# An encoder block on one NeuronCore: in-place squares and low parts of x first in the opening, and the loads of h spread between the operand loads of the second FFN layer

## The chip, the cores and the metric

The kernel runs on one core of a Trainium2 chip. Its time is the device time of one execution, in microseconds (us). Of the kernel before there are three timed runs (1366.92, 1367.37 and 1368.26 us) and one profiled execution. A measurement of this kernel can tell a difference of about 0.2% (2.7 us) from none.

The engines are TensorE (PE, matrix products; its weight loads are listed apart as PEld), VectorE (DVE), ScalarE (ACT), GpSimd (POOL) and SyncE (SP, which here issues all the DMAs). Each engine works through its own list of instructions in the order in which the program issues them; an instruction whose inputs are not there holds up everything behind it on that engine.

## The reference

One layer (DEPTH = 1) for x of 1024 tokens by 1024 features, all in float32:

```python
xn = rmsnorm(h, norm_mix[l]);  proj = xn @ w_in[l]          # q, k, v, u, vs, gates
att = chunked_rel_attention(q, k, v, att_rel_bias[l])
sgu = spatial_gating(gelu(u), gelu(vs), ...)
merged = gates[:, :, 0] * (att @ w_br_att[l]) + gates[:, :, 1] * (sgu @ w_br_sgu[l])
h = h + merged @ w_out[l]
g, up = split(rmsnorm(h, norm_ffn[l]) @ w_ffn_in[l], 2)
h = h + (silu(g) * up) @ w_ffn_out[l]
return rmsnorm(h, norm_final)
```

rmsnorm multiplies each token by the reciprocal root of the mean of its squares, and each feature by a gain.

## The kernel before

Activations lie with features on the 128 partitions and tokens along the row, so x is eight tiles x0 to x7 of 128 features by 1024 tokens (512 KB each). TensorE multiplies in a reduced format, so every operand is split into a high part (ScalarE copies it, rounded) and a low part (what is left, on VectorE or GpSimd), and each product is three matmuls: high by high, high by low, low by high.

**The opening (lines 278 to 431).** For each block x_k, `load_x` issues the load on SP, ScalarE makes the high part `xh` of x_k times the gain (line 289) and VectorE the low part `xl` (line 290). `square_x` makes the square of x_k in a tile of its own (ScalarE, or GpSimd for k = 2 and 3, lines 296 and 298), and VectorE adds it to `acc` (line 300). On VectorE the additions stand between the low parts: `xl` of block k, then the addition for block k-2. `load_first` loads the first weights of q and k in three pieces (blocks 0 and 1, 2 and 3, 4 to 7) and splits them, low parts on GpSimd. The weights of v are four pieces `wv` of two blocks each. They are loaded through the two buffers tagged `raw`, which the first weights of q and k hold until their low parts are made; the low parts of the first two pieces are made on GpSimd, those of the last two on VectorE. The load of x7 comes behind that of the first `wv` in SP's list.

TensorE first runs 18 transposes of nothing, then for each block k twelve matmuls of 512 columns (line 346): q and k, two halves of the tokens, three passes. From the second block on the order is pass by pass, the one with `xl` second. Then come the eight token tiles of v (line 356, 24 matmuls each, reading `wv` piece by piece). Within tile 0, after `SUM_AT` = 12 of its matmuls, TensorE sums `acc` over the partitions (`ss`, line 269, 16 instructions), and a short chain on VectorE and GpSimd (lines 254 to 262 and 411) makes the reciprocal root `rstd_tok`. Within tile 1, after `SPREAD_AT` = 8 matmuls, TensorE spreads it over the partitions (line 275), ScalarE copies it (line 416) and VectorE takes the finished q and k out of their PSUM banks (lines 374 and 376). Tile 2 of v uses the bank of `q0a`, the first half of q.

**The second FFN layer (lines 1507 to 1527).** The activations of the first layer went through DRAM (`act_dram`), the h of before the FFN too (`h_dram`), and the prepared weights as well (`g_dram`, 84 operands of 384 KB). The layer is one list `order_g` of 84 products, nine matmuls of 512 columns each. Operand i lies in one of six buffers; `prepare_g(i + 6)` in step i issues the load of operand i+5 (line 1433), which waits until product i-1 has read that buffer. Operands 0 to 5 and product 0 come earlier, within the first layer's last steps. Between that and the loop stand four loads of h, 1 MB each (line 1485), into a pool that takes the place of the first layer's. The results are added to h by `collect_g`; the first that does so is that of product 8. In steps 8 to 13 one load of 512 KB each brings the next six activations (`stage_act`, line 1399), from which VectorE, ScalarE and GpSimd make the next right-hand operands (lines 1416, 1419 and 172).

Of the kernel before, what the change touches and what calls it, by code (L numbers as in the profile page):

```python
# [11 lines left out]
F32 = mybir.dt.float32  # L12
F32R = mybir.dt.float32r
AF = mybir.ActivationFunctionType
OP = mybir.AluOpType

P = 128
D = 1024
S = 1024
KB = D // P  # L20
# [16 lines left out]
LOW_G = ((0, 1, 1, 1, 0, 1, 0, 1, 1, 1, 0, 1, 0, 1, 1, 1, 0, 1, 0, 1, 1), (1, 0, 0, 0, 0, 1, 1, 0, 1, 0, 0, 1, 0, 0, 1, 0, 1, 1, 0, 0, 1))  # L37
SHARES = (((4, 5), (4, 4)), ((4, 3), (4, 4)), ((4, 3), (6, 4)), ((4, 4), (3, 3)))
WAKE = 18
SUM_AT, SPREAD_AT = 12, 8  # L40
EPS = 1e-6
NEG = -1e30
GELU_A = 0.044715
# [4 lines left out]
def encoder_block(ctx: ExitStack, tc: tile.TileContext, xT, w_in, w_v, w_vs, w_att, w_sgu, w_out,  # L48
# [5 lines left out]
    nc = tc.nc  # L54
# [3 lines left out]
    wpool = ctx.enter_context(tc.tile_pool(name="wpool", bufs=2))  # L58
# [10 lines left out]
    def slot(name, shape=(P, S), dt=F32, pool=slots):  # L69
        return pool.tile(list(shape), dt, name=name, tag="slot")  # L70
# [4 lines left out]
    halves = (slice(0, HALF), slice(HALF, S))  # L75
# [145 lines left out]
    for j in range(PAIRS):  # L221
        qw[j] = block(f"wq{j}", w_in[j], D)
        kw[j] = block(f"wk{j}", w_in[4 + j], D)
        if j == 0:
            vw = [block(f"wv{i}", w_v[i], D, keep=two_slots, lo_engine=nc.vector if i >= 2 else None) for i in range(4)]
        for g in {1: (0,), 2: (1,), 3: (2, 3)}.get(j, ()):
            uw[g] = block(f"wu{g}", w_in[8 + g], D)
    gw, bw = [], {}
# [11 lines left out]
    g_mix, g_ffn, g_fin, b_gate = vec[:, 0:8], vec[:, 8:16], vec[:, 16:24], vec[:, 24:40]  # L240
# [35 lines left out]


    xg = []
    acc = slot("acc")

    def load_x(k, parts=1):

        x.append(slot(f"x{k}"))
        xg.append((slot(f"xh{k}", dt=F32R), slot(f"xl{k}", dt=F32R)))
        for s in halves if parts == 2 else (slice(0, S),):
            nc.sync.dma_start(x[k][:, s], xT[k * P:(k + 1) * P, s])
            yield 1
            hi, lo = (part[:, s] for part in xg[k])
            nc.scalar.activation(hi, x[k][:, s], AF.Copy, scale=g_mix[:, k:k + 1])
            nc.vector.scalar_tensor_tensor(lo, x[k][:, s], g_mix[:, k:k + 1], hi.bitcast(F32),  # L290
                                           op0=OP.mult, op1=OP.subtract)

    def square_x(k):
        q = acc if k == 0 else slot(f"xq{k}")
        if k in POOL_SQUARES:
            nc.gpsimd.tensor_tensor(out=q, in0=x[k], in1=x[k], op=OP.mult)
        else:
            nc.scalar.activation(q, x[k], AF.Square)
        if k:
            nc.vector.tensor_tensor(out=acc, in0=acc, in1=q, op=OP.add)  # L300

    def load_first(c0, c1):
        s = slice(c0 * P, c1 * P)
        for u in (qw[0], kw[0]):
            if c0 == 0:
                for part in ("raw", "hi", "lo"):
                    u[part] = wpool.tile([P, D], F32 if part == "raw" else F32R, name=u["name"] + part, tag=part)
            nc.sync.dma_start(u["raw"][:, s], u["src"][:, s])
        yield 1
        for u in (qw[0], kw[0]):  # L310
            hi, lo, raw = (u[part][:, s] for part in ("hi", "lo", "raw"))
            nc.scalar.copy(hi, raw)
            nc.gpsimd.tensor_tensor(out=lo, in0=raw, in1=hi.bitcast(F32), op=OP.subtract)
# [1 line left out]
    awake = wide_ps("awake", "s")[:, :P]  # L315
    warm = small.tile([P, 1], F32, name="warm", tag="warm", bufs=1)
    nc.scalar.activation(warm, ones, AF.Square)
    POOL_SQUARES = (2, 3)
    x = []
    first_x, first_w = load_x(0, 2), load_first(0, 2)  # L320
    next(first_x)
    next(first_w)
    next(first_x)
    drain(first_w, first_x, load_x(1), load_first(2, 4))
    for k in range(2, KB):
        drain(load_x(k))
        square_x(k - 2)
        if k == 2:
            drain(load_first(4, KB))
            state["dma"] = state["split"] = 2  # L330
        if k >= 6:
            split_to(k - 3)
    square_x(KB - 2)
    square_x(KB - 1)
    dma_to(6)
    split_to(6)


    for _ in range(WAKE):
# [1 line left out]
    first = [dense_ps("q0a"), dense_ps("q0b"), *(wide_ps(f"k0{n}", "v", (P, HALF)) for n in "ab")]  # L341
    for k in range(KB):
        of_k = [(i, half, n) for i in range(2) for n in range(3) for half in range(2)]
        for i, half, n in of_k if k else sorted(of_k, key=lambda x: x[1]):
            w, b = passes((qw, kw)[i][0], k, xg[k])[n]
            nc.tensor.matmul(first[2 * i + half], w, b[:, halves[half]], start=k == 0 and n == 0,
                             stop=k == KB - 1 and n == 2)

    def project(ps, pieces, t):

# [5 lines left out]
                nc.tensor.matmul(ps, a, b, start=k == 0 and n == 0, stop=k == KB - 1 and n == 2)  # L356
                yield

    dma_to(6)
    split_to(6)  # L360
    v = [slot(f"v{i}", (P, HEADS, 2, DH), F32R) for i in range(NT)]
    rstd = slot("rstd")
    rstd_tok = const.tile([P, NT], F32, name="rstd_tok")
# [25 lines left out]
    def k_evac(o):  # L389
        return head_evac(o, "ka", "kb")  # L390
# [15 lines left out]
    for t in range(NT):  # L406
        ps = dense_ps(f"v{t}") if t > 1 else two[:, t]
        matmuls = project(ps, vw, t)
        if t == 0:
            take(matmuls, SUM_AT)  # L410
            nc.vector.tensor_copy(rstd_tok, inverse_rms("rms1", sum_features("ss1", acc, NT, "t"), NT))
        elif t == 1:
            take(matmuls, SPREAD_AT)
            ps2 = wide_ps("rstd1", "t")
            spread(rstd_tok, ps2, NT)
            nc.scalar.copy(rstd, ps2)
            for evac, tiles in ((q_evac(qk[0]), first[:2]), (k_evac(qk[0]), first[2:])):
                for half in range(2):
                    drain(evac(half, halves[half], tiles[half]))
            drain(turn_queries(0, 0))  # L420
        drain(matmuls)
        if t and t % 2 == 0:
            dma_to(6 + t // 2)
            split_to(5 + t // 2)
        for n in {0: (), 1: (0, 1)}.get(t, (t,)):
            hi, lo = (v[n][:, :, part] for part in range(2))
            ps = (two[:, n] if n < 2 else ps).rearrange("p (h d) -> p h d", h=HEADS)
            nc.scalar.activation(hi, ps, AF.Copy, scale=rstd_tok[:, n:n + 1])
            nc.vector.scalar_tensor_tensor(lo, ps, rstd_tok[:, n:n + 1], hi.bitcast(F32),
                                           op0=OP.mult, op1=OP.subtract)  # L430
# [171 lines left out]
    with tc.tile_pool(name="apool", bufs=2) as apool:  # L602
# [7 lines left out]
        for i in range(len(steps) + 2):  # L610
            if i % (2 * NT) == 0 and i < len(steps):
                j = i // (2 * NT)
# [440 lines left out]
    h_dram = dram.tile([KB, P, S], F32, name="h_dram")  # L1053
# [38 lines left out]
    raws, sums, parts, state_f, low_f = {}, {}, {}, {"next": 0}, []  # L1092
# [50 lines left out]
    acc = [ftmp("acc0"), ftmp("acc1")]  # L1143
# [54 lines left out]
    for i, (j, half) in enumerate(order_w):  # L1198
        n = i - 12
# [174 lines left out]
    for i in range(last_pair - 5):  # L1374
# [12 lines left out]
        if i >= MAKE_FROM:  # L1387
# [6 lines left out]
                lo_engine=nc.vector if j == 1 else None) for j in range(KB)]  # L1394
# [71 lines left out]
    for i in range(last_pair - 5, len(order)):  # L1466
        f = i - last_pair + 5
# [13 lines left out]
    h_all = gpool.tile([P, KB, S], F32, name="h_all", tag="h")  # L1481
    h = [h_all[:, j] for j in range(KB)]
    first_g = gpool.tile([P, 4, HALF], F32, name="first_g", tag="first")
    for j in range(0, KB, 2):
        nc.sync.dma_start(h_all[:, j:j + 2], h_dram[j:j + 2].rearrange("k p t -> p k t"))
    later = [i for i in range(8) if order_g[i][2] == "2"]
    for i, (c, r, p) in enumerate(order_g):
        n = i - 28 * c
        prepare_g(i + 6)
        if i:  # L1490
            product_g(i)
        if i not in later:
            collect_g(i)
        if n == i and 12 <= i < 16:
            collect_g(later[i - 12])
        f = n - (5 if c else 8)
        if 0 <= f < 6 and 6 * (c + 1) + f < FB:
            stage_act(6 * (c + 1) + f)
        if c + 1 < PARTS:
            if n == (12 if c else 14):  # L1500
                coming = operands_g(c + 1)
        elif n in (12, 15, 18, 21):
            split_act(6 * PARTS + (n - 12) // 3)
        take(coming, TAKE_G[i] if i < len(TAKE_G) else 1)
        if i == len(order_g) - 4:
            split_to(units.index(fo[0]) + 1)
# [3 lines left out]
    acc = slot("acc3")  # L1510
# [32 lines left out]
    for i, (a, b) in enumerate(token_parts):  # L1543
        s = slice(a, b)
# [62 lines left out]
```

## Time and profile before

| | us |
|---|---|
| median of 3 runs (lowest, highest) | 1367.37 (1366.92, 1368.26) |
| profiled execution | 1366.99 |
| its span | 1365.3 |
| PE busy | 1319.1 (97% of the span) |
| DVE, ACT, POOL busy | 922.6, 569.2, 526.3 |
| HBM read and written | 125.33 MB, 52.95 MB |

The span runs from the first to the last instruction; the execution's own time is 1.7 us longer. A busy PE is not a PE at its full clock: the granted clock is listed apart, as a share of 2.4 GHz (1.00 is 2.4 GHz, 0.50 is 1.2 GHz). "L346" is line 346 of the kernel before.

### The profile page before, as it was taken

The page shows a single profiled execution, that of the slowest core. Times are in us where ns is not written, and L with a number is a line of the kernel's source. Part 1 is how long each engine was busy: PE and PEld are TensorE (multiplying, and loading weights), DVE is VectorE, ACT ScalarE, POOL GpSimd, SP SyncE. Part 2 cuts the span into 40 slices and gives each one's busy share as a digit, 9 for nine tenths or more (in the row PEclk, how much of TensorE's full clock was granted, in tenths as well). Part 3 has the DMA queues.
Part 4 walks back from the last instruction along what each step waited for, and adds up shares of the span by engine and source line. Part 5 has one row for each costly group of instructions (what it writes and reads, how often), then busy time and mean ns, then how long its engine had stood idle before and what let it go on. Part 6 is the DMA issues. An engine that isn't in the chain of part 4 may idle for free.

```text
span 1365.3 us, 17376 instructions
## 1 busy us (share of the span) xinstructions
PE 1319.1 (97%) x6290; PEld 1093.8 (80%) x6290; DVE 922.6 (68%) x1449; ACT 569.2 (42%) x1054; POOL 526.3 (39%) x406
## 2 busy tenths in 40 slices
PE   7999999999998999999987999999999998999997
PEld 5888888878886777888875788888888886888887
DVE  6347777771869778762279777787787755757445
ACT  6236656663434544442243344344444333212144
POOL 5425444324457345434366322312222222323332
PEclk9999999999999999999988999999999998999998
DMA  6011010103041111253111365666566558786723
GB/s 216 31 43 37 19 39 17 37 22 101 17 162 39 62 54 61 71 207 147 62 47 62 144 215 189 226 216 225 191 215 227 196 191 296 251 283 201 249 63 124
DMA packets 65782, 179.42 MB, mean 131 GB/s; under 512 B 7200, under 2 KB 10784, under 8 KB 65696
## 3 DMA queue, kind: packets, MB, share of 16 engines
q1 hardware_dynamic: 65696, 178.31, 37.9%
q8 instruction: 50, 0.82, 0.2%
q14 instruction: 36, 0.29, 0.1%
HBM read 125.33 MB, written 52.95 MB: 131 GB/s over the span
## 4 chain that ended last, share of the span: by engine, by line
PE 56%; DVE 5%; DMA 1%; issue 1%; ACT 0%; POOL 0%; SPq 0%; DVEq 0%; ACTq 0%; POOLq 0%
PE c L181 39%; PE wo L1173 6%; PE mc L181 5%; PE last L167 3%; PE mp L181 2%; DMA g<-g_dram 1%; DVE s L1108 0%; DMA fu<-in_w_ffn_in 0%; DVE b L1321 0%; DVE t L1311 0%; DVE b22l L172 0%; DVE t L1304 0%; DMA g_dram<-g 0%; PE bc L275 0%; DVE b L1079 0%
## 5 line engine op out<-in xcount | busy, mean ns | idle before, releaser
L1136 POOL TENSOR_TENSOR w_lo<-s,w_hi 128x512 fp32r<-128x512 f32 x70 | 107.1, 1536 | 270.0 <-ACT w_hi L1130 267.3
L181 PE MATMUL c<-t,g 128*128 128x512 f32 x432 | 102.7, 390 | 0.0
L1130 ACT CAST w_hi<-s 128x512 fp32r<-128x512 f32 x88 | 54.6, 620 | 108.1 <-DVE s L1108 104.5
L181 PEld LDWEIGHTS c<-t,g 128*128 128x128 f32 x432 | 81.1, 188 | 17.0 <-DVE t L172 0.2
L1455 DVE TENSOR_TENSOR h_all<-h_all,c 128x512 f32<-128x512 f32 x72 | 49.1, 687 | 61.2 <-PE c L181 60.4
L181 PE MATMUL c<-b,g 128*128 128x512 f32 x324 | 81.2, 399 | 6.1 <-DMA g<-g_dram 6.1
L181 PEld LDWEIGHTS c<-b,g 128*128 128x128 f32 x324 | 62.7, 194 | 19.7 <-ACT t L1419 6.4
L478 ACT ACTIVATE p<-p,low 128x640 f32<-128x640 f32 (+4 forms) x64 | 44.6, 697 | 58.6 <-DVE low L470 58.4
L1419 ACT CAST t<-stage 128x512 fp32r<-128x512 f32 x36 | 22.2, 622 | 86.6 <-DVE stage L1416 81.2
L155 POOL TENSOR_TENSOR wm_lo<-wg,wm_hi 128x512 fp32r<-128x512 f32 x21 | 30.7, 1464 | 63.4 <-ACT wm_hi L154 59.5
L172 POOL TENSOR_TENSOR t<-stage,t 128x512 fp32r<-128x512 f32 x18 | 26.3, 1465 | 64.5 <-ACT t L1419 55.4
L1173 PE MATMUL wo<-mergedhi,wo_hi 128*128 128x512 f32 x128 | 50.0, 391 | 0.0
L1173 PE MATMUL wo<-mergedhi,wo_lo 128*128 128x512 f32 x128 | 49.9, 390 | 0.0
L1173 PE MATMUL wo<-mergedlo,wo_hi 128*128 128x512 f32 x128 | 49.9, 390 | 0.0
L470 DVE CUSTOM_DVE_ANT_0 p<-s,bias 128x640 f32<-128x640 f32 (+4 forms) x64 | 41.7, 652 | 10.8 <-PE s L466 8.8
L496 DVE TENSOR_TENSOR ptl<-t,pth 128x640 fp32r<-128x640 f32 (+4 forms) x64 | 41.7, 651 | 4.5 <-ACT pth L495 4.3
L167 PE MATMUL last<-act_hi,fo 128*128 128x256 f32 (+1 forms) x192 | 43.8, 320 | 0.0
L1364 ACT CAST g<-fo 128x384 fp32r<-128x384 f32 x60 | 30.5, 509 | 29.8 <-issue 14.8
L480 DVE TENSOR_SCALAR p<-p,inv 128x640 f32<-128x640 f32 (+4 forms) x64 | 39.6, 619 | 2.2
L1338 DVE TENSOR_TENSOR g<-fo,g 128x384 fp32r<-128x384 f32 x60 | 39.8, 663 | 0.0
L1178 DVE TENSOR_TENSOR h<-h,wo 128x512 f32<-128x512 f32 x16 | 11.0, 688 | 41.6 <-PE wo L1173 41.6
L489 PE MATMUL t<-ident,p 128*128 128x128 f32 x240 | 37.0, 274 | 1.8 <-DVE ptl L496 1.6
(426 smaller groups left out, 4277.7 us busy)
## 6 DMA issues: line engine op xcount, KB each, us to landing
g_dram<-g SPq DMA_DIRECT2D x84, 384.0 KB, 2.5
g<-g_dram SPq DMA_DIRECT2D x84, 384.0 KB, 3.5
fg<-in_w_ffn_in SPq DMA_DIRECT2D x22, 512.0 KB, 4.1
fu<-in_w_ffn_in SPq DMA_DIRECT2D x22, 512.0 KB, 4.2
act_dram<-u SPq DMA_DIRECT2D x44, 256.0 KB, 2.4
stage<-act_dram SPq DMA_DIRECT2D x22, 512.0 KB, 6.2
fo<-in_w_ffn_out SPq DMA_DIRECT2D x24, 384.0 KB, 4.3
xn<-in_xT SPq DMA_DIRECT2D x8, 512.0 KB, 8.5
```

The costliest lines, as they stand in the source:

```text
L167: nc.tensor.matmul(ps, w, x[:, s], start=k == 0 and i == 0, stop=k == kc - 1 and i == 2)
L181: nc.tensor.matmul(ps, w[:, ws], x, start=first and k == 0 and n == 0, stop=k == last and n == 2, skip_group_check=True)
L470: nc.vector.tensor_tensor_reduce(out=p[:, :w].rearrange("p (a c) -> p a c", a=parts), in0=ps[:, :parts, :c], in1=bias.rearrange("p (a c) - ...
L478: nc.scalar.activation(e["p"], e["p"], AF.Exp, bias=e["low"], scale=-1.0, accum_out=e["tot"])
L480: nc.vector.tensor_scalar(e["p"], e["p"], e["inv"], None, op0=OP.mult)
L489: nc.tensor.transpose(ps[:, b * P:(b + 1) * P], e["p"][:, b * P:(b + 1) * P], ident)
L496: nc.vector.tensor_tensor(out=lo[:, :w], in0=ps[:, :w], in1=hi[:, :w].bitcast(F32), op=OP.subtract)
L1130: nc.scalar.copy(hi, src)
L1136: nc.gpsimd.tensor_tensor(out=lo, in0=src, in1=hi.bitcast(F32), op=OP.subtract)
L1173: nc.tensor.matmul(banks_w[j, half], w, x, start=k == 0 and n == 0, stop=k == KB - 1 and n == 2, skip_group_check=True)
L1338: nc.vector.tensor_tensor(out=t[:, W3:2 * W3], in0=src, in1=t[:, :W3].bitcast(F32), op=OP.subtract)
L1455: nc.vector.tensor_tensor(out=dst, in0=dst, in1=banks_g[name, r], op=OP.add)
```

## The change

In the opening, all loads of x are issued ahead of those of `wv`, and the loads of the first two `wv` pieces go into slots of their own instead of the `raw` buffers. ScalarE squares every block in place, and VectorE adds the squares into x0; no separate tiles for squares are left, and GpSimd makes none. The low parts of x stand earlier in VectorE's list than nearly all additions, and the low parts of all four `wv` pieces are made on VectorE. TensorE takes the passes with `xl` last in every block from the second on. The sum of the squares moves from tile 0 of v (after 12 matmuls) to tile 1 (after 6), and the spreading comes 12 matmuls behind it. In the second FFN layer the four loads of h are issued in steps 0, 3, 5 and 7 of the loop, and the six loads of activations of part 0 in steps 8, 9, 11, 12, 13 and 14.

```diff
+H_AT, STAGE_AT = (0, 3, 5, 7), (8, 9, 11, 12, 13, 14)
-SUM_AT, SPREAD_AT = 12, 8
+SUM_AT, SPREAD_AT = 6, 12
...
-            vw = [block(..., lo_engine=nc.vector if i >= 2 else None) for i in range(4)]
+            vw = [block(..., lo_engine=nc.vector) for i in range(4)]
...
             nc.sync.dma_start(x[k][:, s], xT[k * P:(k + 1) * P, s])
             yield 1
-            hi, lo = (part[:, s] for part in xg[k])
-            nc.scalar.activation(hi, ...)
-            nc.vector.scalar_tensor_tensor(lo, ...)
+            if parts == 2:
+                scale_x(k, s)
+
+    def scale_x(k, s=slice(0, S)):
+        hi, lo = (part[:, s] for part in xg[k])
+        nc.scalar.activation(hi, x[k][:, s], AF.Copy, scale=g_mix[:, k:k + 1])
+        nc.vector.scalar_tensor_tensor(lo, x[k][:, s], g_mix[:, k:k + 1], hi.bitcast(F32), op0=OP.mult, op1=OP.subtract)

     def square_x(k):
-        q = acc if k == 0 else slot(f"xq{k}")
-        if k in POOL_SQUARES:
-            nc.gpsimd.tensor_tensor(out=q, in0=x[k], in1=x[k], op=OP.mult)
-        else:
-            nc.scalar.activation(q, x[k], AF.Square)
-        if k:
-            nc.vector.tensor_tensor(out=acc, in0=acc, in1=q, op=OP.add)
+        nc.scalar.activation(x[k], x[k], AF.Square)
+
+    def add_x(k):
+        nc.vector.tensor_tensor(out=x[0], in0=x[0], in1=x[k], op=OP.add)
+
+    def load_v(i):
+        u = vw[i]
+        u["raw"] = wpool.tile([P, D], F32, ..., tag="raw") if i > 1 else slot(u["name"] + "_raw")
+        nc.sync.dma_start(u["raw"], u["src"])
...
-    drain(first_w, first_x, load_x(1), load_first(2, 4))
-    for k in range(2, KB):
-        drain(load_x(k))
-        square_x(k - 2)
-        if k == 2:
-            drain(load_first(4, KB))
-            state["dma"] = state["split"] = 2
-        if k >= 6:
-            split_to(k - 3)
-    square_x(KB - 2)
-    square_x(KB - 1)
-    dma_to(6)
+    drain(first_w, first_x, load_x(1))
+    more_w = load_first(2, 4)
+    next(more_w)
+    drain(load_x(2))
+    last_w = load_first(4, KB)
+    next(last_w)
+    drain(*(load_x(k) for k in range(3, KB)))
+    scale_x(1)
+    drain(more_w)
+    scale_x(2)
+    square_x(0)
+    drain(last_w)
+    for i in range(4):
+        load_v(i)
+    state["dma"], state["split"] = 6, 2
+    scale_x(3)
+    square_x(1)
+    scale_x(4)
+    scale_x(5)
+    add_x(1)
+    scale_x(6)
+    scale_x(7)
+    split_to(3)
+    square_x(2)
+    split_to(4)
+    square_x(3)
+    add_x(2)
+    split_to(5)
+    square_x(4)
+    add_x(3)
     split_to(6)
+    for k in range(5, KB):
+        square_x(k)
+        add_x(k - 1)
+    add_x(KB - 1)
+    acc = x[0]
...
-        for i, half, n in of_k if k else sorted(of_k, key=lambda x: x[1]):
+        for i, half, n in sorted(of_k, key=lambda x: x[2] == 1 if k else x[1]):
...
-        if t == 0:
+        if t == 1:
             take(matmuls, SUM_AT)
             nc.vector.tensor_copy(rstd_tok, inverse_rms("rms1", sum_features("ss1", acc, NT, "t"), NT))
-        elif t == 1:
             take(matmuls, SPREAD_AT)
...
-    for j in range(0, KB, 2):
-        nc.sync.dma_start(h_all[:, j:j + 2], h_dram[j:j + 2].rearrange("k p t -> p k t"))
...
-        f = n - (5 if c else 8)
+        if i in H_AT:
+            j = 2 * H_AT.index(i)
+            nc.sync.dma_start(h_all[:, j:j + 2], h_dram[j:j + 2].rearrange("k p t -> p k t"))
+        f = n - 5 if c else STAGE_AT.index(i) if i in STAGE_AT else -1
```

## Rows read from the trace of the kernel before

**Rows 1.** Waits of PE over the span: total us, times, longest.

```profile
PE q0a L346 <- DVE xl L290: 5.3, 3, 2.7
```

**Rows 2.** Stretches of the opening: us; busy PE, PEld, DVE, ACT, POOL; clock; DMA; GB/s.

```profile
14.00:16.00 2.00, 2.00 (x10) 1.66 (x9) 1.20 (x1) 2.00 (x3) 2.00 (x3) 1.00 1.10 418
24.00:26.00 2.00, 2.00 (x6) 1.52 (x6) 2.00 (x2) 2.00 (x3) 2.00 (x2) 0.50 0.14 16
```

**Rows 3.** Timeline of PE, opening: start us, us, instruction, [idle before, releaser].

```profile
9.80 0.50 PE L346 MATMUL q0a<-xh,wq0hi 128*128 128x512 f32 x1 [0.23 <-ACT xh L289]
...
22.66 0.50 PE L346 MATMUL q0a<-xl,wq0hi 128*128 128x512 f32 x1 [2.65 <-DVE xl L290]
...
36.01 0.39 PE L346 MATMUL q0a<-xh,wq0hi 128*128 128x512 f32 x1
...
38.73 0.39 PE L356 MATMUL v<-wv_hi,xh 128*128 128x512 f32 x1
```

**Rows 4.** Timeline of DVE, opening.

```profile
9.79 1.28 DVE L290 SCALAR_TENSOR_TENSOR xl<-x,vec,xh 128x1024 fp32r<-128x1024 f32 x1 [1.70 <-ACT xh L289]
...
14.80 2.14 DVE L290 SCALAR_TENSOR_TENSOR xl<-x,vec,xh 128x1024 fp32r<-128x1024 f32 x1 [1.35 <-ACT xh L289]
...
25.87 3.37 DVE L290 SCALAR_TENSOR_TENSOR xl<-x,vec,xh 128x1024 fp32r<-128x1024 f32 x1
...
30.30 1.27 DVE L290 SCALAR_TENSOR_TENSOR xl<-x,vec,xh 128x1024 fp32r<-128x1024 f32 x1
...
33.82 3.87 DVE L300 TENSOR_TENSOR acc<-acc,xq 128x1024 f32<-128x1024 f32 x3
37.61 2.35 DVE L124 TENSOR_TENSOR wv_lo<-wv_raw,wv_hi 128x1024 fp32r<-128x1024 f32 x2
```

**Rows 5.** Timeline of ACT, opening.

```profile
10.58 1.15 ACT L289 ACTIVATE xh<-x,vec 128x1024 fp32r<-128x1024 f32 x1 [0.23 <-DMA x<-in_xT]
...
13.62 1.15 ACT L289 ACTIVATE xh<-x,vec 128x1024 fp32r<-128x1024 f32 x1
...
15.62 3.22 ACT L289 ACTIVATE xh<-x,vec 128x1024 fp32r<-128x1024 f32 x3
```

**Rows 6.** Timeline of POOL, opening.

```profile
14.56 1.30 POOL L313 TENSOR_TENSOR wk0lo<-wk0raw,wk0hi 128x512 fp32r<-128x512 f32 x1
...
21.49 6.67 POOL L124 TENSOR_TENSOR wv_lo<-wv_raw,wv_hi 128x1024 fp32r<-128x1024 f32 x2
```

**Rows 7.** Timeline of SP's issues, opening.

```profile
6.53 2.88 SPq L286 DMA_DIRECT2D x<-in_xT  x4
...
14.99 0.43 SPq L286 DMA_DIRECT2D x<-in_xT  x1
```

**Rows 8.** Timeline of all engines, sum of squares and spreading.

```profile
41.22 1.98 PEld L269 LDWEIGHTS ss<-ones,acc 128*128 128x128 f32 x16
...
45.92 0.17 DVE L411 COPY rstd_tok<-rms_y 128x8 f32<-128x8 f32 x1
...
47.60 1.01 PEld L275 LDWEIGHTS rstd<-ident,rstd_tok 128*128 128x128 f32 x8
...
49.94 0.69 DVE L376 SCALAR_TENSOR_TENSOR qkt<-q0a,rstd 128x512 f32<-128x512 f32 x1 [3.85 <-ACT rstd L416]
```

**Rows 9.** Timeline of PE and SP, start of the second FFN layer.

```profile
1130.07 2.05 SPq L1485 DMA_DIRECT2D h_all<-h_dram  x4
1132.16 19.59 SPq L1433 DMA_DIRECT2D g<-g_dram  x8
...
1144.41 6.99 PE L181 MATMUL c<-b,g 128*128 128x512 f32 x18 [6.05 <-DMA g<-g_dram]
1151.24 6.29 PE L181 MATMUL c<-t,g 128*128 128x512 f32 x27
```

**Rows 10.** Loads of h (tile h_all, 1128 to 1152 us): times from issue to landing.

```profile
DMA to landing us min/median/max: 5.3/8.7/11.8
```

**Rows 11.** One stretch of the second layer's start, columns as in rows 2.

```profile
1144.40:1151.24 6.84, 6.83 (x19) 5.39 (x19) 0.00 (x0) 0.58 (x1) 1.06 (x1) 0.59 0.76 278
```

More of the change, by code (lines that the diff above doesn't have):

```diff
@@ L224, in encoder_block @@
         if j == 0:
-            vw = [block(f"wv{i}", w_v[i], D, keep=two_slots, lo_engine=nc.vector if i >= 2 else None) for i in range(4)]
+            vw = [block(f"wv{i}", w_v[i], D, keep=two_slots, lo_engine=nc.vector) for i in range(4)]
         for g in {1: (0,), 2: (1,), 3: (2, 3)}.get(j, ()):
@@ L278, in encoder_block @@
     xg = []
-    acc = slot("acc")
     def load_x(k, parts=1):
@@ L284, in load_x @@
         xg.append((slot(f"xh{k}", dt=F32R), slot(f"xl{k}", dt=F32R)))
-        for s in halves if parts == 2 else (slice(0, S),):
+        pieces = halves if parts == 2 else (slice(0, S),)
+        for s in pieces:
             nc.sync.dma_start(x[k][:, s], xT[k * P:(k + 1) * P, s])
             yield 1
-            hi, lo = (part[:, s] for part in xg[k])
-            nc.scalar.activation(hi, x[k][:, s], AF.Copy, scale=g_mix[:, k:k + 1])
-            nc.vector.scalar_tensor_tensor(lo, x[k][:, s], g_mix[:, k:k + 1], hi.bitcast(F32),
-                                           op0=OP.mult, op1=OP.subtract)
-    def square_x(k):
-        q = acc if k == 0 else slot(f"xq{k}")
-        if k in POOL_SQUARES:
-            nc.gpsimd.tensor_tensor(out=q, in0=x[k], in1=x[k], op=OP.mult)
-        else:
-            nc.scalar.activation(q, x[k], AF.Square)
-        if k:
-            nc.vector.tensor_tensor(out=acc, in0=acc, in1=q, op=OP.add)
+            if parts == 2:
[4 more added lines that the diff above has]
+        nc.vector.scalar_tensor_tensor(lo, x[k][:, s], g_mix[:, k:k + 1], hi.bitcast(F32), op0=OP.mult, op1=OP.subtract)
+    def square_x(k):
+        nc.scalar.activation(x[k], x[k], AF.Square)
[3 more added lines that the diff above has]
+        u = vw[i]
+        u["raw"] = wpool.tile([P, D], F32, name=u["name"] + "_raw", tag="raw") if i > 1 else slot(u["name"] + "_raw")
+        nc.sync.dma_start(u["raw"], u["src"])
     def load_first(c0, c1):
@@ L317, in encoder_block @@
     nc.scalar.activation(warm, ones, AF.Square)
-    POOL_SQUARES = (2, 3)
     x = []
@@ L343, in encoder_block @@
         of_k = [(i, half, n) for i in range(2) for n in range(3) for half in range(2)]
-        for i, half, n in of_k if k else sorted(of_k, key=lambda x: x[1]):
+        for i, half, n in sorted(of_k, key=lambda x: x[2] == 1 if k else x[1]):
             w, b = passes((qw, kw)[i][0], k, xg[k])[n]
             nc.tensor.matmul(first[2 * i + half], w, b[:, halves[half]], start=k == 0 and n == 0,
-                             stop=k == KB - 1 and n == 2)
+                             stop=k == KB - 1 and n == 1)
     def project(ps, pieces, t):
@@ L357, in project @@
                 yield
-    dma_to(6)
-    split_to(6)
     v = [slot(f"v{i}", (P, HEADS, 2, DH), F32R) for i in range(NT)]
```

## The prediction

> **What bounds the kernel now.** I read the page first: PE is busy for 97% of the span, and the chain that ended last is mostly matmuls. So the time is the sum of PE's instructions, and a change pays only where PE stands still or runs at the lower clock. The list of PE's waits says where: the wait for `xl` in the opening is 5.3 us in three pieces [rows 1], and one wait of 6.05 us for operand 6 stands at the start of the second FFN layer [rows 9]. The stretches add what the waits don't show. After the waits of the opening PE had a granted clock of 0.50, which is 1.2 GHz, from 24 to 26 us [rows 2]; after the wait for operand 6 it was 0.59 on the mean, so mostly 1.2 GHz, for 6.84 us [rows 11]. The reader is to see in both places a wait and a slow stretch behind it.
>
> At 2.4 GHz twelve matmuls of 512 columns take 38.73 - 36.01 = 2.72 us, 0.227 us each [rows 3]. From the first matmul of block 1 (9.80) to the first of v (38.73) PE needed 28.93 us [rows 3] for 7 x 12 matmuls worth 19.04 us: 9.89 us are lost there.
>
> The loss comes from VectorE's list. An `xl` alone takes 1.27 us; beside GpSimd at work on two 1024-column low parts (6.67 us) one took 3.37 us [rows 4, 6]. And an addition stands ahead of each, so block 4's `xl` let PE wait 2.65 us [rows 3].
>
> **The opening, first half: to the end of q and k (gain 9.89 us).** Block 0 is unchanged. Block k (1 to 7) can now start at 9.80 + 2.72 (k - 1), needs `xh` then and `xl` 8 x 0.227 = 1.82 us later, since its four `xl` matmuls come last. If all are in time, q and k end at 9.80 + 19.04 = 28.84.
>
> `xh`: ScalarE's order up to the fifth is as before, so xh2 ends at 11.73 (needed 12.52), xh3 at 14.77 (15.24), xh4 at 15.62 + 1.15 = 16.77 (17.96), xh5 at about 17.8 (20.68), xh6 at 18.84 (23.40) [rows 5]. xh7 follows at about 20.0 (26.12): x7's load was issued at 14.99 behind a wait, and now goes right behind that of x6 at about 9.4 [rows 7]. x6 was there when its xh began at about 17.7, and 0.52 MB more at 418 GB/s [rows 2] are 1.3 us, so x7 is there by 19.0.
>
> `xl`: xl1 ends at 11.07 (needed 11.62), xl3 at 16.94 or earlier (17.06) [rows 4]; that is the closest one. From xl4 on GpSimd is idle, since its last low part ends at 15.86 [rows 6] and squares and `wv` are taken from it. xl4 ends at 16.77 + 1.27 = 18.04 (needed 19.78), xl5 at 19.31 (22.5), and after one addition xl6 at 21.8 (25.2), xl7 at 23.0 (27.9). The low parts of q's and k's weights are as before.
>
> What a GpSimd operation does to one on VectorE decides xl3. The row has 2.14 us beside the low part that ends at 15.86 [rows 4, 6]. The Trainium skill ("SBUF — State Buffer", Who interferes with whom) says that a VectorE instruction with two SBUF inputs and a GpSimd instruction that reads SBUF exclude each other for a whole instruction. By that xl3 would end at 15.86 + 1.27 = 17.13 (an estimate from that page and the rows), 0.07 us late for PE, against nothing by the row; by the row the two overlap a little.
>
> **The opening, second half: v (loses 1.0 us).** The low part of `wv` piece 2 is needed at 28.84 + 12 x 0.227 = 31.6, piece 3 at 32.9. The four loads follow x7 at 1.3 us each, the last by about 24.3 (the two that wait for a `raw` buffer have it at 15.86 [rows 6]); ScalarE's copies stand at about 20, 22, 24 and 26 between squares of 1.0 us. VectorE goes on at 23.0 with four low parts and two additions at 2.35 / 2 = 1.18 us [rows 4]: 30.1, so `wv` costs nothing. Four additions on each other follow at 3.87 / 3 = 1.29 us [rows 4]: x0 is complete at 35.3. PE asks for it after 24 + 6 matmuls of v, at 28.84 + 6.81 = 35.65. The cover is 0.35 us; what goes beyond is a wait of PE.
>
> From the first `ss` weight load to `rstd_tok` it is 46.09 - 41.22 = 4.87 us [rows 8]. PE fills 1.9 us of `ss` and 12 x 0.227, together 4.62, so the spreading waits 0.25. From its start to the end of taking `q0a` out of PSUM it is 50.63 - 47.60 = 3.03 us [rows 8]. Until now 16 matmuls of tile 1 lay in there; now there are 6, so PE asks for that bank for tile 2 at 1.0 + 1.36 = 2.36 us and waits some 0.75 us with the semaphore. That wait is new. Its bounds are 0 (if another bank were free) and the whole 0.75; I take 0.75, as tile 2 has the bank of `q0a`. The in-place squares wait for `xl` of the same block, at the closest xl1 at 11.07 against 14.67: nothing. The opening as a whole gives 9.89 - 1.0 = 8.9 us, and all behind it, which follows PE, shifts by that.
>
> **The second FFN layer (gain 8.8 us).** PE's wait is 6.05 us; then 18 matmuls took 1151.24 - 1144.41 = 6.83 us instead of 18 x 0.227 = 4.09 [rows 9]. Together 6.05 + 2.74 = 8.79 us. The four loads of h landed 5.3 to 11.8 us after their issue at 1130.07 and later, one after the other [rows 9, 10]; operand 6, issued behind all four at 1132.16, came at about 1144.3. A model of that: 2 us, then 410 GB/s in the order of issue. It gives 1130.2 + 2 + (0.26 + 1.05) / 0.41 = 1135.4 for the first load of h (the 0.26 MB are a store before it); the row has 1130.07 + 5.3 = 1135.4.
>
> Now operand 6 stands behind one load of h: 1136.4, and product 6 is due at 1144.41 - 6.05 = 1138.36. With the loads of SP's new order, each product 2.04 us later: operand 9 at 1141.8 (due 1144.5), 11 at 1146.3 (1148.6), 13 at 1150.7 (1152.6), 15, behind all h and two loads of activations, at 1155.2 (1156.7), 20 at 1165.1 (1166.9). The least cover is 1.5 us. The last h lands at 1149.8; it is first read in step 15, at about 1156. No load waits for more than before, so SP's list holds nothing new. The activations are read from step 14 on (1154.7); the first of them lands at 1152.0. The right-hand operands of products 8 to 12 are made during the wait of now: VectorE had nothing left to do from 1144.40 on [rows 11], and product 8 is due at 1142.4. It loses 2.0 us if it needs the last of these operands and nothing if it needs the first; its operand t2 is made first, so I take nothing. If the loads shared the engines instead of following each other, operand 6 would have at worst 3.9 MB ahead: 3.4 us late. The row of landings speaks against it.
>
> **Sum.** 8.9 + 8.8 = 17.7 us off the profiled execution's 1366.99: 1349.3. The median is 0.38 above it, so 1349.7.
>
> **The rivals.**
>
> A. Sum of squares late. If VectorE's 14 operations behind xl4 took 1.70 us each, midway between the 1.27 alone and the 2.14 of an overlap [rows 4], x0 would be complete at 18.04 + 14 x 1.70 = 41.84, 6.2 us after PE asks, and PE would go on at 1.2 GHz for at least the 2 us of [rows 2], half of them lost, 1.0 us: the opening gives 8.9 - 7.2 = 1.7 us, time 1356.9. For it: twenty operations in one list, and 0.35 us of cover. Against: rows of VectorE with GpSimd idle are all 1.3 us or less.
>
> B. Operands late in the second layer. At 350 GB/s instead of 410 operand 15 comes 9.43 / 0.35 = 26.9 us after 1132.2, 2.4 late, and the lower clock costs about 2 more: gain 4.4, time 1354.1. For it: from step 8 to 14 each step asks for 0.39 and mostly 0.52 MB in 2.04 us, more than 410 GB/s. Against: operands are asked for five products ahead.
>
> C. Slower than before: each load of h stops PE once. Four waits of 2.6 us (1.05 MB), each with the 2.74 us of low clock, are 21.4 us against the 8.8 of now; with the opening's gain 1371.1. It decides from where an operand behind a load of h lands after its product is due; that is 1.9 us off for operand 6.
>
> D. The change doesn't do what it says in the second layer: operand 6 is as late as before because the engines work on all loads together. Then only the opening stays: 1358.5.
>
> **How the numbers follow.** Forecast 0.70, A 0.10, B 0.12, C 0.04, D 0.04. The forecast's own bounds are 1348.7 (without the two short waits of v) and about 1353 (`ss` and two operands a little late). The range goes from 1347.0, as other waits can shrink too, to 1356.5; it leaves out A, C and D, 0.18. About 0.2% (2.7 us) is what can be told from no change: faster by more than that 0.95 (forecast, A, B, D, less a little for what I don't see), within it 0.01, slower 0.04 (C).
>
> **What would show it.** First matmul of v at about 28.8 and granted clock 1.00 from 10 to 60 us: first half. A wait before `rstd` (line 275) of about 0.25 and one before tile 2 of v of about 0.75: second half. `ss` waiting for `acc` for more than 1 us: A. No wait for `g<-g_dram` and clock 1.00 from 1128 to 1170 (then some 9 us earlier): second layer; several short ones at steps 13 to 20: B, one behind each load of h: C. The prediction is wrong if x7 or `wv` land after 20 to 26 us, or if a stage behind the opening takes longer than before.

## The result, and the profile after

The changed kernel takes 1349.56 us (median of 4 runs, 1349.28 to 1350.34) against 1367.14 (1366.87 to 1368.26) for the kernel before on the same chip: a ratio of 0.9871, 95% interval 0.9854 to 0.9888, 17.6 us less. The forecast was 1349.7. The profiled execution took 1349.5 us with a span of 1347.8 us; the profiled execution before had a span of 1365.3.

The page of the kernel after, its first part, columns as in the table of before: engine, busy us and share, instructions.

```profile
PE 1312.0 (97%) x6290; PEld 1088.4 (81%) x6290; DVE 921.2 (68%) x1451; ACT 571.8 (42%) x1056; POOL 513.4 (38%) x402
```

The opening and the layer's start after, as stretches (columns as in [rows 2]):

```profile
10.00:60.00 50.00, 49.49 (x230) 40.72 (x229) 28.85 (x31) 28.90 (x36) 21.08 (x18) 1.00 0.32 123
1119.31:1150.31 31.00, 30.98 (x137) 25.18 (x135) 24.49 (x33) 11.41 (x21) 7.32 (x5) 1.00 0.93 362
```

The granted clock is 1.00 in both, so nothing of the 1.2 GHz of before is left there.

PE's timeline of the opening after, which answers to [rows 3]: start us, us, instruction, [idle before, releaser].

```profile
10.37 0.40 PE L375 MATMUL q0a<-xh,wq0hi 128*128 128x512 f32 x1
...
29.43 0.39 PE L385 MATMUL v<-wv_hi,xh 128*128 128x512 f32 x1
...
36.24 1.84 PE L270 MATMUL ss<-ones,x 128*128 128x1 f32 x16
...
41.03 1.06 PE L276 MATMUL rstd<-ident,rstd_tok 128*128 128x128 f32 x8
...
43.09 0.40 PE L385 MATMUL v<-wv_hi,xl 128*128 128x512 f32 x1
43.92 0.50 PE L385 MATMUL v<-wv_hi,xh 128*128 128x512 f32 x1 [0.44 <-DVE qkt L403]
...
76.71 0.22 PE L491 MATMUL s<-ka,qa 128*128 128x128 f32 x1
```

The reader is to see that blocks 1 to 7 now take 29.43 - 10.37 = 19.06 us, with no bracket between; before it was 28.93 [rows 3]. The bracket at 43.92 is new: tile 2 of v waits for its bank. VectorE's timeline after answers to [rows 4], and GpSimd's last low part to [rows 6]:

```profile
14.98 4.53 DVE L295 SCALAR_TENSOR_TENSOR xl<-x,vec,xh 128x1024 fp32r<-128x1024 f32 x3 [1.35 <-ACT xh L294]
19.43 1.21 DVE L302 TENSOR_TENSOR x<-x,x 128x1024 f32<-128x1024 f32 x1
20.56 2.47 DVE L295 SCALAR_TENSOR_TENSOR xl<-x,vec,xh 128x1024 fp32r<-128x1024 f32 x2
22.95 2.35 DVE L125 TENSOR_TENSOR wv_lo<-wv_raw,wv_hi 128x1024 fp32r<-128x1024 f32 x2
...
29.77 5.21 DVE L302 TENSOR_TENSOR x<-x,x 128x1024 f32<-128x1024 f32 x4
```

```profile
14.74 1.29 POOL L320 TENSOR_TENSOR wk0lo<-wk0raw,wk0hi 128x512 fp32r<-128x512 f32 x1
```

All of x0 is summed at 29.77 + 5.21 = 34.98, and PE asks for it at 36.24. The start of the second FFN layer after, PE and its weight loads, answers to [rows 9]:

```profile
1119.31 14.44 PE L182 MATMUL c<-b,g 128*128 128x512 f32 x63
1133.59 6.28 PE L182 MATMUL c<-t,g 128*128 128x512 f32 x27
1139.71 2.20 PE L182 MATMUL c<-b,g 128*128 128x512 f32 x9
1141.75 8.72 PE L182 MATMUL c<-t,g 128*128 128x512 f32 x36
1150.31 2.21 PE L182 MATMUL c<-b,g 128*128 128x512 f32 x9
```

```profile
1145.79 1.91 PEld L182 LDWEIGHTS c<-t,g 128*128 128x128 f32 x9 [0.23 <-DMA g<-g_dram]
1148.12 1.92 PEld L182 LDWEIGHTS c<-t,g 128*128 128x128 f32 x9 [0.42 <-issue]
```

The first row is products 1 to 7, which run through, so the wait of 6.05 us and the slow stretch behind it are gone. From its start to that of product 8 it is 1133.59 - 1119.31 = 14.28 us; before, with product 1 at 1128.00 in the same view, it was 1151.24 - 1128.00 = 23.24. What remains are two short brackets at products 14 and 15: the 36 matmuls of products 12 to 15 take 1150.31 - 1141.75 = 8.56 us for 36 x 0.227 = 8.17.

SP's timeline and the landings of the loads of h after, which answer to [rows 9, 10], and one stretch of it (busy time of PE, PEld, DVE, ACT and POOL; granted clock; DMA share; GB/s):

```profile
1121.38 0.38 SPq L1522 DMA_DIRECT2D h_all<-h_dram  x1
1121.81 2.09 SPq L1459 DMA_DIRECT2D g<-g_dram  x3
1123.95 0.58 SPq L1522 DMA_DIRECT2D h_all<-h_dram  x1
```

```profile
DMA to landing us min/median/max: 5.6/9.5/10.4
```

```profile
76.71:1119.31 1042.60, 1018.61 (x4887) 843.03 (x4885) 745.57 (x1193) 464.77 (x886) 412.52 (x317) 0.99 0.33 115
```

That stretch is all that lies between the two places: 1042.60 us from the first score of the attention to product 1 of the second layer; before, that score stood at 85.01 in PE's timeline, so it was 1128.00 - 85.01 = 1042.99. So the gain of the span is 85.01 - 76.71 = 8.30 us in the opening, 0.39 between, and 8.96 at the layer's start, less 0.4 given back at products 14 and 15: 17.25 of the 17.5. The other 0.25 lies behind the start of product 16, at 1167.57 of 1365.3 before and at 1150.31 of 1347.8 after.

### The profile page after: what moved, and what is told of

It is laid out like the page before. It is cut to its first block, busy times and chain, and to the rows that moved or that the text cites. A ratio compares the mean times of both kernels' runs of the same rounds, so it can differ in the third digit from the quotient of the medians.

```text
span 1347.8 us, 17376 instructions
## 1 busy us (share of the span) xinstructions
PE 1312.0 (97%) x6290; PEld 1088.4 (81%) x6290; DVE 921.2 (68%) x1451; ACT 571.8 (42%) x1056; POOL 513.4 (38%) x402
## 4 chain that ended last, share of the span: by engine, by line
PE 57%; DVE 5%; issue 1%; ACT 1%; POOL 0%; DMA 0%; DVEq 0%; ACTq 0%; POOLq 0%
PE c L182 41%; PE wo L1199 6%; PE mc L182 5%; PE last L168 3%; PE mp L182 2%; DVE s L1134 0%; DVE b L1347 0%; DVE t L1337 0%; DVE b22l L173 0%; DVE t L1330 0%; DMA g_dram<-g 0%; DVE b L1105 0%; DVE t2l L173 0%; DVE b22f L1105 0%; DVE mergedlo L781 0%
## 5 line engine op out<-in xcount | busy, mean ns | idle before, releaser
L182 PEld LDWEIGHTS c<-t,g 128*128 128x128 f32 x432 | 80.9, 188 | 17.5 <-issue 0.4
L182 PE MATMUL c<-b,g 128*128 128x512 f32 x324 | 78.3, 389 | 0.0
```

What stands on the lines that cost most here:

```text
L182: nc.tensor.matmul(ps, w[:, ws], x, start=first and k == 0 and n == 0, stop=k == last and n == 2, skip_group_check=True)
```

## The experiments

All ratios are to the kernel before on the same chip, with the 95% interval. All kernels compute the whole reference. All edits are shown against the changed kernel, cut at `...`.

**Each part alone.** opening_only puts the layer's loads back; layer_only puts the opening back.

```diff
+    for j in range(0, KB, 2):
+        nc.sync.dma_start(h_all[:, j:j + 2], h_dram[j:j + 2].rearrange("k p t -> p k t"))
...
-        if i in H_AT:
...
-        f = n - 5 if c else STAGE_AT.index(i) if i in STAGE_AT else -1
+        f = n - (5 if c else 8)
```

> The changed opening with the second FFN layer as before (four loads of h in a row, activations in steps 8 to 13). If the two parts add up: before (1367.1) less 8.3 to 8.7 us, so 1358.4 to 1358.9, with one wait for g<-g_dram of about 6 us and a stretch of about 7 us at a granted clock near 0.6 behind it, as before. Rival: the second layer alone makes the gain, or the stages between give the opening's gain back; then 1363 or more.

1357.76 us, 0.9932 (0.9917 to 0.9946): 8.8 us gained. The wait in the layer is back in PE's list of waits and in its timeline:

```profile
PE c L182 <- DMA g<-g_dram: 6.0, 1, 6.0
```

```profile
1134.05 6.37 PE L182 MATMUL c<-b,g 128*128 128x512 f32 x18 [6.03 <-DMA g<-g_dram]
```

```diff
-SUM_AT, SPREAD_AT = 6, 12
+SUM_AT, SPREAD_AT = 12, 8
...
-            vw = [block(f"wv{i}", w_v[i], D, keep=two_slots, lo_engine=nc.vector) for i in range(4)]
+            vw = [block(f"wv{i}", w_v[i], D, keep=two_slots, lo_engine=nc.vector if i >= 2 else None) for i in range(4)]
...
+        q = acc if k == 0 else slot(f"xq{k}")
...
```

> The opening as before with the changed second FFN layer (loads of h in steps 0, 3, 5, 7; activations in steps 8, 9, 11 to 14). If the parts add up: before (1367.1) less 8.4 to 8.9, so 1358.2 to 1358.7; no wait of PE for g<-g_dram over 0.5 us, granted clock 1.00 there; the three waits for xl in the opening as before (5.3 us). Rival: the layer only gains behind the new opening; then 1363 or more.

1359.12 us, 0.9944 (0.9929 to 0.9958): 7.4 us gained, about 1 less than expected and within the interval. From product 1 to the end it takes 1358.3 - 1129.71 = 228.6 us, against 1365.3 - 1128.00 = 237.3 before, so the layer gave 8.7. Its span is only 7.0 shorter: of the 1.7 us between, 0.8 stand ahead of v, with waits for `xl` 1.5 us longer than in [rows 1], and 0.9 between v and the layer. Its list has the wait for `xl` and none for `g`:

```profile
PE q0a L347 <- DVE xl L291: 6.8, 3, 3.6
```

0.9932 x 0.9944 = 0.9876 against 0.9871 for both: the two parts add up and do nothing to each other.

**Why `xl` was late: GpSimd's share, or the order of VectorE's list.** pool_shares keeps the new order and gives GpSimd its squares and low parts again.

```diff
+            vw = [block(f"wv{i}", w_v[i], D, keep=two_slots, lo_engine=nc.vector if i >= 2 else None) for i in range(4)]
...
+        if k in (2, 3):
+            nc.gpsimd.tensor_tensor(out=x[k], in0=x[k], in1=x[k], op=OP.mult)
...
```

> The changed kernel with GpSimd given back its share of the opening: squares of blocks 2 and 3 (in place) and the low parts of the first two wv pieces; VectorE's list loses those two low parts and keeps its order otherwise. If GpSimd's work beside VectorE is what stretched VectorE's list: from about 16 to 28.5 us each VectorE operation of 1024 columns takes 2.9 to 3.4 us, the low part of block 6 ends at about 30 instead of 21.8, PE waits for it some 4 us and loses 1 to 2.7 more at the lower clock: 1354 to 1358. Rival, that the order of VectorE's list is the cause: GpSimd's work is harmless behind the new order, 1349 to 1351.

1356.52 us, 0.9922 (0.9907 to 0.9937): 7.0 us slower than with the whole change. The size is as expected, the place is not. There is no wait for an `xl` of blocks 1 to 7; the waits stand behind q and k. First PE's list, then VectorE's and GpSimd's timelines, then one stretch:

```profile
PE ss L270 <- DVE x L305: 2.3, 1, 2.3
...
PE v L388 <- DVE wv_lo L125: 1.6, 2, 1.0
```

```profile
20.44 4.63 DVE L295 SCALAR_TENSOR_TENSOR xl<-x,vec,xh 128x1024 fp32r<-128x1024 f32 x2
26.86 3.41 DVE L305 TENSOR_TENSOR x<-x,x 128x1024 f32<-128x1024 f32 x1 [1.79 <-POOL x L300]
...
33.02 1.21 DVE L305 TENSOR_TENSOR x<-x,x 128x1024 f32<-128x1024 f32 x1
```

```profile
20.97 3.01 POOL L125 TENSOR_TENSOR wv_lo<-wv_raw,wv_hi 128x1024 fp32r<-128x1024 f32 x1 [5.07 <-ACT wv_hi L123]
...
26.78 2.40 POOL L125 TENSOR_TENSOR wv_lo<-wv_raw,wv_hi 128x1024 fp32r<-128x1024 f32 x1
29.14 2.88 POOL L300 TENSOR_TENSOR x<-x 128x1024 f32<-128x1024 f32 x1
```

```profile
42.00:44.00 2.00, 2.00 (x11) 2.00 (x11) 0.00 (x0) 0.00 (x0) 0.00 (x0) 0.50 0.00 0
```

An addition that takes 1.21 us alone first waits 1.79 us for GpSimd's square and then takes 3.41 beside GpSimd's low part, and the sum of squares is late by 2.3 us. That is rival A of the prediction, brought about by GpSimd: waits of 3.9 us, and then 1.2 GHz. The Trainium skill ("SBUF — State Buffer", Who interferes with whom) would have the addition run after GpSimd's instruction, 29.18 + 1.21 = 30.39 (an estimate by its rule); it ended at 30.27. So the trace agrees with the rule but for 0.12 us of an overlap.

This run doesn't put GpSimd's work where it stood before, though. There its squares began at 15.82:

```profile
15.82 5.71 POOL L296 TENSOR_TENSOR xq<-x 128x1024 f32<-128x1024 f32 x2
```

Here, in place and further back in its list, they leave GpSimd idle from 15.90 to 20.97, while VectorE makes `xl` of blocks 4 and 5. Of the two `xl` at 20.44 only the last one was stretched (4.63 us for both instead of 2.47), and PE wanted that one only at about 28.

old_list does the converse: before's order on VectorE and ScalarE, GpSimd left idle.

```diff
...
+    for k in range(3, KB):
+        scale_x(k)
+        square_x(k - 2)
+        add_x(k - 2)
+        if k >= 6:
+            split_to(k - 3)
...
```

> The changed kernel with the order of before on VectorE and ScalarE (square and addition of block k-2 behind the scaling of block k, low parts of the last two wv pieces behind all additions), but GpSimd still idle there. If GpSimd is the cause of the loss: an addition of 1.2 us between low parts of 1.3 us makes 2.5 us a block, less than PE's 2.72, so PE waits for no xl; only the low part of wv piece 2 ends at about 33.6, due at 32.2: 1350.5 to 1351.5. Rival, that the order of the list is the cause: waits for xl come back, 1354 or more.

1352.0 us, 0.9891 (0.9874 to 0.9907): 2.4 us slower than the whole change, some 1 more than expected, but less than the 2.7 us that times can tell. Again no wait for `xl` in blocks 1 to 7; one wait in v, for the last low parts of `wv`, which the old order leaves until 32.37 (PE's list, VectorE's timeline):

```profile
PE v L375 <- DVE wv_lo L125: 1.2, 1, 1.2
```

```profile
32.37 2.35 DVE L125 TENSOR_TENSOR wv_lo<-wv_raw,wv_hi 128x1024 fp32r<-128x1024 f32 x2
```

So neither half of the edit, put back alone, brings the waits for `xl` back; of the next two runs xl_second brings back 1.0 us and old_loads nothing. Only layer_only, which puts back the whole opening, has them. Which parts together make them is not shown: both runs keep the new order of PE's passes and the early loads, and in pool_shares GpSimd also starts later. What either half costs stands in v: from its first matmul to the first score it is 55.02 us in pool_shares and 48.77 in old_list, against 47.28 with the whole change. GpSimd's share is the costlier half.

**The order of PE's passes.** xl_second leaves the `xl` matmuls of a block second, as before.

```diff
-        for i, half, n in sorted(of_k, key=lambda x: x[2] == 1 if k else x[1]):
+        for i, half, n in of_k if k else sorted(of_k, key=lambda x: x[1]):
...
```

> The changed kernel with TensorE's order of before in each block of the opening (pass by pass, the one with xl second). xl is then needed 0.45 us into a block instead of 1.82. With the ends of xl1 and xl3 in the changed kernel (11.25 and about 16.9) PE waits about 0.4 for xl1 and 0.2 for xl3, nothing for the others: 0.4 to 0.8 us slower than the changed kernel, 1350.0 to 1350.4. Rival, that the order of the passes is what took the waits away: three waits of 1 to 3 us, 1354 or more.

1350.2 us, 0.9881 (0.9866 to 0.9896). Blocks 1 to 7 took 20.10 us instead of 19.06, from nearly the same start (10.38 and 10.37): the order is worth 1.0 us there, and no more.

**The loads of x7 and `wv`.** old_loads has them in before's slots and order.

```diff
-        u["raw"] = wpool.tile([P, D], F32, name=u["name"] + "_raw", tag="raw") if i > 1 else slot(u["name"] + "_raw")
+        u["raw"] = wpool.tile([P, D], F32, name=u["name"] + "_raw", tag="raw")
...
+    load_v(0)
+    drain(load_x(KB - 1))
+    load_v(1)
...
```

> The changed kernel with the loads of the opening as before: all four wv pieces through the two raw buffers, x7's load behind that of the first piece, the last two behind the low parts of the first two. x7 lands at about 20.5 instead of 17.5, ScalarE's list shifts by some 2 us, the last wv low part ends at about 32 (due 33.5), the sum of squares at about 35.3 (due 36.0): 0 to 0.5 us slower than the changed kernel. Rival, that the early loads are needed: wv or x0 late by more than 1 us and PE at the lower clock, 1352 or more.

1353.89 us, 0.9907 (0.9892 to 0.9922): 4.3 us slower than the whole change, where I expected at most 0.5. The rival was right. SP, ScalarE, VectorE and PE, then the clock:

```profile
16.15 9.75 SPq L307 DMA_DIRECT2D wv_raw<-in_w_v  x3
```

```profile
27.75 1.05 ACT L123 CAST wv_hi<-wv_raw 128x1024 fp32r<-128x1024 f32 x1 [2.51 <-DMA wv_raw<-in_w_v]
```

```profile
23.05 2.50 DVE L125 TENSOR_TENSOR wv_lo<-wv_raw,wv_hi 128x1024 fp32r<-128x1024 f32 x2
...
28.84 1.23 DVE L125 TENSOR_TENSOR wv_lo<-wv_raw,wv_hi 128x1024 fp32r<-128x1024 f32 x1 [2.16 <-ACT wv_hi L123]
...
32.25 5.21 DVE L302 TENSOR_TENSOR x<-x,x 128x1024 f32<-128x1024 f32 x4
```

```profile
37.51 2.63 PE L270 MATMUL ss<-ones,x 128*128 128x1 f32 x16 [1.37 <-DVE x L302]
```

```profile
38.00:40.00 2.00, 2.00 (x14) 2.00 (x14) 0.00 (x0) 0.00 (x0) 0.00 (x0) 0.64 0.00 0
40.00:42.00 2.00, 2.00 (x6) 1.61 (x7) 0.17 (x1) 0.00 (x0) 1.51 (x1) 0.50 0.00 0
42.00:44.00 2.00, 2.00 (x7) 1.52 (x6) 0.67 (x4) 0.00 (x0) 0.14 (x1) 0.50 0.00 0
44.00:46.00 2.00, 2.00 (x11) 1.60 (x10) 0.00 (x0) 0.00 (x0) 0.00 (x0) 0.65 0.00 0
```

The loads of pieces 2 and 3 wait for the two `raw` buffers until VectorE has made the low parts of pieces 0 and 1 (23.05 to 25.55): they are issued at 24.29 and 25.57, with the whole change at 14.80 and 16.06. So ScalarE's copy of piece 2 waits 2.51 us, VectorE with it, and x0 is summed at 37.46 instead of 34.98. I had the end of the last low part right (about 32; it was 32.33), but put the sum at 35.3, though four additions of 5.21 us stand behind it. PE stands 1.37 us, and then runs at 1.2 GHz or between the two levels until 46: 0.72 + 1.00 + 1.00 + 0.70 = 3.4 us of work that it does not do. 1.4 + 3.4 = 4.8, near the 4.3 measured: the price of a wait of 1.4 us was mostly the clock behind it.

**The spacing of the loads of h.** h_dense issues one per step in steps 0 to 3.

```diff
-H_AT, STAGE_AT = (0, 3, 5, 7), (8, 9, 11, 12, 13, 14)
+H_AT, STAGE_AT = (0, 1, 2, 3), (8, 9, 11, 12, 13, 14)
```

> The changed kernel with the loads of h in steps 0, 1, 2 and 3. If transfers follow each other in the order of issue at about 410 GB/s: operand 7 stands behind two loads of h and comes about 1.1 us late, operands 8 and 9 about 1.4 each; about 4.0 us in three waits of PE, and, if waits of that length lower the clock, up to 3 more: 1353 to 1357. Rival, that the engines share their time among all loads in flight: the smaller operands overtake the loads of h, waits under 1 us in all, 1349.5 to 1350.5.

1352.52 us, 0.9895 (0.9878 to 0.9911): 3.0 us slower than the whole change. PE's timeline:

```profile
1134.78 2.35 PE L182 MATMUL c<-t,g 128*128 128x512 f32 x9 [1.14 <-DMA g<-g_dram]
1138.32 4.63 PE L182 MATMUL c<-t,g 128*128 128x512 f32 x18 [1.18 <-DMA g<-g_dram]
```

Operands 8 and 9 are late, and the time lies between the two theories, nearer that of loads which follow each other. The landings say the same: all of these loads landed in the order of issue. The granted clock stayed at 1.00 from 1128 to 1155, so these waits cost themselves only.

**The slots of the activations.** stage_old has their loads in steps 8 to 13.

```diff
-H_AT, STAGE_AT = (0, 3, 5, 7), (8, 9, 11, 12, 13, 14)
+H_AT, STAGE_AT = (0, 3, 5, 7), (8, 9, 10, 11, 12, 13)
```

> The changed kernel with the six loads of activations in steps 8 to 13 as before. In the changed kernel operands 14 and 15 land 0.2 and 0.4 us late. One more load of activations (0.52 MB, 1.3 us) then stands ahead of operands 16 to 20, whose cover is about 1 us: 0.2 to 1.0 us slower than the changed kernel, in waits of PE for g<-g_dram at products 16 to 18. Rival: the cover there is larger and nothing changes (within 0.2 us).

1350.26 us, 0.9877 (0.9862 to 0.9892). By time it can't be told from the whole change. Its trace has products 12 to 15 at 8.72 us instead of 8.56 and product 16 at 2.37 instead of 2.04: 0.5 us, the size expected.

**The four short waits that are left.** closer asks for the sum of squares four matmuls of v earlier and for the spreading one matmul later behind it, and moves the first two loads of activations one step later.

```diff
-H_AT, STAGE_AT = (0, 3, 5, 7), (8, 9, 11, 12, 13, 14)
-SUM_AT, SPREAD_AT = 6, 12
+H_AT, STAGE_AT = (0, 3, 5, 7), (9, 10, 11, 12, 13, 14)
+SUM_AT, SPREAD_AT = 2, 13
```

> The changed kernel with the four small waits that its trace shows aimed at: sum of squares after 2 instead of 6 matmuls of tile 1 of v and spreading 13 instead of 12 behind it (so 9 instead of 6 matmuls of tile 1 cover the way to the bank of q0a), activations of part 0 in steps 9 to 14 (one load less ahead of operands 14 and 15). Waits: 0.2 before the spreading and 0.6 before tile 2 of v go to under 0.2 together, 0.23 and 0.42 at products 14 and 15 go to 0: 1.0 to 1.3 us faster than the changed kernel, 1348.3 to 1348.6. Rival: the sum of squares is not ready after 2 matmuls, and the wait moves there: no gain, 1349.5 or more.

1348.44 us, 0.9865 (0.9846 to 0.9883), the lowest of all, though its 1.1 us to the whole change are within what the times can tell. Its trace is plainer (PE at the layer's start):

```profile
1140.26 8.36 PE L182 MATMUL c<-t,g 128*128 128x512 f32 x36
1148.46 2.20 PE L182 MATMUL c<-b,g 128*128 128x512 f32 x9
```

Products 12 to 15 take 1148.46 - 1140.26 = 8.20 us, and from v's first matmul to the first score it is 46.47 us instead of 47.28. The brackets are gone: 0.36 + 0.81 = 1.2 us.

## Why the prediction was right

**The sum.** 17.7 us off the profiled execution were forecast, 17.5 came, and each half came from its place: 8.9 forecast and 8.30 found in the opening, 8.8 and 8.96 at the layer's start. opening_only and layer_only show that the halves are independent. That the sum fits within 0.2 us is partly luck: with this same opening v began between 28.43 and 29.63 us in other executions, as the first loads landed.

**q and k, 9.89 us: right.** 28.93 - 19.06 = 9.87. The agreement to 0.02 is chance: in opening_only, h_dense, stage_old and closer, with the same code up to there, these blocks took 19.05 to 19.85 us. The closest cover was named: xl3. It ran from 14.98 beside a GpSimd low part that ended at 16.03. The three `xl` end at 19.51 and two alone take 2.47 us (the row at 20.56), so the second began at 17.04; each begins 0.07 before the one ahead of it ends (2 x 1.27 - 2.47), so xl3 ended at about 17.11. By the Trainium skill ("SBUF — State Buffer", Who interferes with whom) it would have been 16.03 + 1.27 = 17.30, an estimate. The measurement decides for the small overlap that the prediction took from its row, 0.19 us there (15.86 + 1.27 - 16.94) and here. Either would have done, by luck: block 1 started late, and PE asked for xl3 only at 10.37 + 5.44 + 1.82 = 17.63; from the start that was forecast it would have asked at 17.06.

**Block 0 unchanged: off by 0.57.** Block 1 started at 10.37 instead of 9.80, because the second half of x0 landed later (its `xh` began at 7.55; before, 6.58). The opening's 8.30 is 9.87 - 1.00 - 0.57. It need not be the change: with the same opening, block 1 started at 8.71 in opening_only, 9.78 in closer and 9.94 in pool_shares.

**v, a loss of 1.0: right.** From v's first matmul to the first score it is 47.28 us after and 85.01 - 38.73 = 46.28 before. `rstd_tok` was done at 40.88 and the spreading started at 41.03, 0.2 us later than it could have for PE (0.25 named). The bank of `q0a` kept PE for about 0.6 of the 0.75: the matmuls stand at 43.09 and 43.92 where they follow at 0.227. VectorE worked its list off as forecast (the last `xl` by 23.03 for 23.0, x0 at 34.98 for 35.3); as v started 0.59 later than forecast, x0's cover was 36.24 - 34.98 = 1.26 us instead of 0.35.

**"`wv` costs nothing": right for this change, but by a cover that I had wrong.** I put it down to the four loads following x7, and in old_loads' expectation took their slots to be worth 0.5 us at most. They are worth 4.3.

**The layer, 8.79: right.** One load of h ahead of operand 6 didn't delay it, and the products that followed ran at 2.4 GHz. The right-hand operand t2, taken at nothing, cost nothing: product 8 follows without a bracket.

**The least cover of 1.5 us: wrong.** Operands 14 and 15 landed at 1145.7 and 1148.0, right before the weight loads that waited for them, where the model, applied to the issue times after, gives 1144.3 and 1146.5; they were late by 0.23 and 0.42 us. The step that failed is the model's one rate for all engines together. Columns as in the stretches above:

```profile
1121.38:1125.00 3.62, 3.62 (x18) 3.00 (x17) 3.34 (x7) 3.12 (x6) 0.00 (x0) 1.00 0.81 243
1121.38:1145.75 24.37, 24.37 (x109) 20.05 (x107) 20.08 (x27) 10.79 (x19) 6.03 (x4) 1.00 1.00 384
```

The rate was not too low. By 1125.00 the engines had moved 3.62 x 243 = 880 GB/s us, 0.88 MB, where the model, which moves nothing in its first 2 us, has 0.6 MB. By 1145.75 they had moved 24.37 x 384, 9.36 MB, where the store, operand 14 and all loads between are 8.5 MB. So the engines together were ahead of the model while the load was late, and part of them must have lagged behind the rest.

Load by load, the lateness against the model comes in steps: 0.3 us at the first load of h, 0.8 from operand 6 on, 1.4 from the third load of h on, and hardly more behind it. At the last step the queues hold, from 1134.36 us, a packet that is none of the kernel's loads. In the microsecond from 1134 (queue, kind: packets, MB, share of 16 engines):

```profile
q8 instruction: 1, 0.02, 6.7%
```

It has 16 KB, and 6.7% of 16 engines' microsecond is 1.07 us of one engine. All nine runs that issue the loads of h within the loop have this packet at the layer's start, and in each the first load to land more than 2 us after its beginning is where the lateness steps up: by 0.5 us here, by 1.1 to 1.4 us in the eight others, be it the third load of h or operand 10. No run removes the packet, so its part is read from the traces and not shown by an edit. Of the first two steps the cause stays open.

So rival B's lower steady rate is not what happened, though its sign, short waits from product 14 on, was there for 0.4 us. Rival D is out: no wait stands before product 6.

## What to carry to other kernels

When an engine is busy for 97% of the time, read its waits as pairs: the wait, and the stretch at 1.2 GHz that may follow it. A late operand can come from what another engine does beside its maker: here giving GpSimd its share back cost 7.0 us, and giving VectorE its old order 2.4. Before calling a load free, follow it to its last reader: the slots and the order of loads that no engine seemed to wait for were worth 4.3 us. Space large loads among those that are due, and keep more cover than the steady rate of all engines gives: one packet on one of them came with 0.5 to 1.4 us of lateness in the loads behind it.

## What the runs showed of the hardware

- A wait of 1.37 us in the opening was followed by granted clocks of 0.64, 0.50, 0.50 and 0.65 (old_loads, 38 to 46 us). Two of 1.14 and 1.18 us in h_dense and one of 1.22 us in old_list's v were followed by 1.00. Behind the first stood 16 matmuls of one column, behind the other three matmuls of 512 columns; whether that makes the difference is not tested.
- The loads at the start of the second FFN layer, all from SP's queue, landed in the order of issue (whole change and h_dense), an operand of 384 KB about 0.98 us and a load of 1 MB about 2.55 us behind the one before it, but for the steps told above.
- A packet of kind instruction, 16 KB, took 1.07 us of one DMA engine (whole change, 1134.36 us), and the loads behind it landed 0.5 us later; in the eight other runs with the loads of h in the loop it was 1.1 to 1.4 us.
- With one and the same opening, block 1 began between 8.71 and 10.37 us, as the first loads landed: 1.66 us, which is more than an edit worth 1 us, so such an edit is read from the stretch behind it.
